# A Trainium2 encoder trunk: decay weights spread over other steps, heads' rows tied to steps, merging in eight banks

## The chip, the cores and the metric

The kernel runs on one core of a Trainium2 chip. The metric is the time of one execution on the device, in microseconds (us). The profile is of one execution of its own; its engines are PE (TensorE), DVE (VectorE), ACT (ScalarE), POOL (GpSimd) and SP (SyncE, which here issues nearly all DMA transfers).

## The reference

Two sequences, of 1024 and of 256 tokens with 1024 channels each, go through one layer with shared weights. In short (the four heads, and the two directions of the mLSTM, are written once):

```python
h = rms_norm(x, norm_g) * (1.0 + scale) + shift          # shift, scale, gate = c @ w_ada + b_ada
cb, cc, cx, cz, q, k, v, o, mz, gpre, gmerge = split_combined(h @ w_in)
y_conv = cb * centred_dwconv3(cc * cx, conv_w, conv_b) * silu(cz)
# mLSTM, in chunks of 128 tokens, forwards and backwards; C, n, m are carried from chunk to chunk
Dlog = where(mask, b[t] - b[s] + i[s], NEG_BIG)            # b: cumulated log of the forget gate
S = (q @ k.T) * exp(Dlog - m_t)
num = S @ v + inter_w * (q @ C)
hm = num / max(abs(den), exp(-m_t))
y_m = sigmoid(o) * rms_norm_per_head(hm_fwd + hm_bwd) * silu(mz)
merged = g_conv * (y_conv @ w_proj_conv) + g_mlstm * (y_m @ w_proj_mlstm)
y = rms_norm(x + gate * (merged @ w_out), final_norm_g)
```

All of it is float32. The kernel reaches that precision by splitting each operand in a high and a low part and summing three products.

## The kernel before

The 1280 tokens are treated together, with the channels on the partitions for the projections. PE's work comes in this order (times from the span's start in the profile):

- **Projections** h @ w_in, until about 1161 us, by a Strassen scheme. `go(k)` does one of some 310 steps: 24 matmuls of 128 x 320 (L810), into an "acc" tile of three PSUM buffers. The step's weights come through `raw` (three buffers, loaded from `w_in`), sums and differences `comb` on DVE (L675) and a split in `wh` on ACT (L320) and `wl` on POOL (L321). DVE empties each product (L719) or ACT copies it (L733). A bank is free again after that.
- Beside them run the gate recurrences (`recurrences`) and, behind those, the **decay weights**: `weights(i)`, 20 of them, at L1243 to L1258. Each is a load of rows of `a_dr` to all partitions, an addition of the mask on POOL (L1251), four exponentials on ACT (L1255) and a store to `ex_dr`. They share four places, two halves of two `big` tiles: `weights(i)` uses the place of `weights(i - 4)`, so its load waits for that store. The loop at L1345 to L1351 sets at which steps they are due. The convolution's steps (`conv_pairs`) come after `ends[8]`.
- **Sweeps**, 1161 to 1446 us, the mLSTM: `Sweep.query` (L1465, qc), `Sweep.state` (L1505, u; L1513 updates C on DVE), scores (L1548) and the rest, 55 loop steps `s`. Between them stand, as filler, 32 units of y_conv @ w_proj_conv (L1713 to L1715, 24 matmuls each; `Filler.unit`), whose weights are loaded and split two units at a time. `load_head(h, n, which)` loads v, q and k of a head in three pieces of 5, 3 and 2 chunks (640, 384 and 256 KB for each of the three).
- **Merging**, 1446 to 1564 us: y_m @ w_proj_mlstm in 16 blocks of two products of 24 matmuls (L1883 to L1885). `merge` takes a PSUM bank for each product, and DVE multiplies it with the gate `th` (L620). The second half of the blocks uses `ym1`, which `second_ym` loads and splits.
- **Final products** with w_out (L1975 to L1977) until the end.

The order of the instructions on each engine is not that of the code. `Board.op` records operations with a duration, a due step (`board.step`), what they wait for, and marks: `low` (when nothing else is ready), `slack` (added to the time at which a result is taken as ready) and `after`. `Board.order` then plays a planned run: it takes the operation that could begin first, and among those within 0.25 us of it the one that is not low and has the earliest step. For a transfer the planned duration is KB divided by `KB_US`. `play()` emits the instructions in this order, one play for the projections, one for the sweeps, one for merging, one for the rest. On the chip each engine works through its own order strictly. SP has eight semaphores in rotation, and its n-th DMA waits until the one eight before it has landed.

Of the kernel before, what the change touches and what calls it, by code (L numbers as in the profile page):

```python
# [9 lines left out]
F32 = mybir.dt.float32  # L10
F32R = mybir.dt.float32r
AF = mybir.ActivationFunctionType
ALU = mybir.AluOpType
# [3 lines left out]
P = 128  # L17
# [165 lines left out]
def encoder_kernel(  # L183
# [1058 lines left out]
    def weights(i):  # L1242

        gx = gcol[:, 0].rearrange("p d h c -> p d (h c)")
        if not weighing:
            weighing.extend(big() for _ in range(2))
        b, c = weighing[i % 2], i // 2 % 2
        place = (b, c)
        abc = (lambda: b[:, c * 4 * P:(c + 1) * 4 * P].rearrange("p (d j s) -> p d j s", d=2, j=2))
        load(256, abc, a_rows[:, 2 * i:2 * i + 2, :].partition_broadcast(P), ["a_dr"], [place])  # L1250
        op("POOL", 1.35, lambda: G.tensor_tensor(out=abc(), in0=abc(), in1=masks[:].unsqueeze(2).to_broadcast([P, 2, 2, P]),  # L1251
                                                 op=ALU.add), r=[place], w=[place], slack=4.0)
        for d in range(2):
            for j in range(2):
                op("ACT", .39, lambda d=d, j=j: A.activation(abc()[:, d, j, :], abc()[:, d, j, :], AF.Exp,  # L1255
                                                             bias=gx[:, d, 2 * i + j:2 * i + j + 1], scale=1.0),
                   r=[place, "pre"], w=[place])
        store(256, ex_dr[i], lambda: b[:, c * 4 * P:(c + 1) * 4 * P], [place])  # L1258


    sts = {n: gate_pair(n, n + 2, max(i - 2, 0), i == 0) for i, n in enumerate((0, 1, 4, 5, 8, 9))}
# [80 lines left out]
    board.step = at[0]  # L1342
    recurrences()

    for n in range(2, KT):  # L1345
        if n > 3:
            for i in range(NH * NC // 2):
                if i * 4 // (NH * NC // 2) == n - 4:
                    board.step = at[0] + 7 * (i * 4 % (NH * NC // 2)) // (NH * NC // 2)
                    weights(i)  # L1350
        advance(ends[n + 1])  # L1351
    advance(ends[9])

    def first_y():
# [32 lines left out]
                b.open = True  # L1387
    board.KB_US, board.FIRST = 385.0, 1.0
    board.play()
    board.KB_US, board.FIRST = Board.KB_US, Board.FIRST  # L1390
    rstack.close()
    sstack.close()
    xstack.close()
# [34 lines left out]
    def piece(c):  # L1428
        return 0 if c < 5 else 1 if c < 8 else 2

    def load_head(h, n, which="qkv", low=True):

        i, (c0, c1) = h % 2, PIECES[n]
        hs, ts_ = slice(h * HD, (h + 1) * HD), slice(c0 * P, c1 * P)
        kb = 128 * (c1 - c0)
        if "v" in which:
            load(kb, lambda: vNs[i][:, c0:c1, 0:HD], v_dr[ts_, hs].rearrange("(c p) d -> p c d", p=P), (), [(vNs[i], n)], low and h > 0)
        for nm, t, src in (("q", qTs[i], qT_dr), ("k", kTs[i], kT_dr)):
            if nm in which:
                load(kb, lambda t=t: t[:, :, ts_], src[hs, ts_].rearrange("(b p) t -> p b t", p=P), (), [(t, n)], low and h > 0)  # L1440

    class Sweep:

# [309 lines left out]
    for s in range(10 * NH + 15):  # L1753
        board.step = s
        if s == 0:
            fills.unit(())
            load_head(0, 2)
        h, c, i = second(s - 3)
        if h is not None and h + 2 < NH and c in (5, 7, 9):
            load_head(h + 2, (5, 7, 9).index(c))  # L1760
        h, i = divmod(s, 10)
        mark = len(board.ops)
        if h < NH:
            c, d = one[h].order[i], one[h].d
            one[h].query(c, lambda h=h, c=c, d=d: kept[h % 2][:, slot(d, c), :], (kept[h % 2], c))
            one[h].state(c)
        if s == 0:
            fills.unit(())
            for n in DOWN[1:]:
                load_head(0, n, "qv")  # L1770
            fills.unit(())
            fills.unit(())
        h, c, i = second(s)
        if h is not None:
            g = c - c % 2
            if i % 2 == 0:
                prs[h, g] = Pairs(h, g, two_[h].d)
            two_[h].query(c, *prs[h, g].inter(c))
            two_[h].state(c)
            prs[h, g].scores(c)  # L1780
            if i % 2:
                prs[h, g].factors()
        h, c, i = second(s - 2)
        if h is not None:
            prs[h, c - c % 2].values(c)
        h, c, i = second(s - 4)
        if h is not None and i % 2 == 0:
            prs[h, c - c % 2].finish()
        if s in (3, 5):
            for h, n in ((0, 0), (1, 2), (1, 1)) if s == 3 else ((1, 0), (0, 1)):  # L1790
                load_head(h, n, "qkv" if h else "k", False)
        after = [o for o in board.ops[mark:] if o.eng == "PE"][:1]
        while fills.at < PACE[s]:
            fills.unit(after)
        if s == 45:
            ym0 = [first_ym(0)]
        if s == 51:
            raws_m = [raw_tile() for _ in range(2)]
            for j, raw in enumerate(raws_m):
                load(512, lambda raw=raw: raw[:], wpm[:, 4 * j:4 * j + 4, 0:2 * P], (), [raw])  # L1800
            ws_m = [split_op(lambda raw=raw: raw[:, :, 0:P], [raw]) for raw in raws_m]
# [8 lines left out]
    bstack.close()  # L1810


    psO = ctx.enter_context(tc.tile_pool(name="psO", bufs=2, space=PSUM))
    psY = hpstack.enter_context(tc.tile_pool(name="psY", bufs=4, space=PSUM))
    mgp = ctx.enter_context(tc.tile_pool(name="mgp", bufs=1))
    zcp = hpstack.enter_context(tc.tile_pool(name="zcp", bufs=5, side="right"))
    def bank():
        b = buf(psY, [P, 512], F32, "acc", 4)
        return b, b

    def mg_half(pool, tags):
# [20 lines left out]
    def second_ym(n):  # L1842
        y = [buf(hp, [P, 4, TH2], F32R, ("b00", "b10")[n] + part, 1) for part in "HL"]
        v = ym_dr[:].rearrange("(k p) t -> p k t", p=P)
        for k in range(4):
            raw = buf(thp, [P, TH2], F32, "th", NTH)
            kt = 4 * n + k
            load(320, lambda raw=raw, kt=kt: raw[:], v[:, kt, 0:TH2], (), [raw], True)
            op("ACT", .8, lambda raw=raw, k=k: A.copy(y[0][:, k], raw[:]), r=[raw], w=[(y[0], k)])
            op("DVE", .83, lambda raw=raw, k=k: V.tensor_tensor(out=y[1][:, k], in0=raw[:], in1=fp(y[0][:, k]),  # L1850
                                                                op=ALU.subtract), r=[raw, (y[0], k)], w=[(y[1], k)])
        return y
# [222 lines left out]
    ym1 = []  # L2075
    for i in range(2 * KT):
        board.step = i
        if i < 6 and i % 2 == 0 and i < 4:
            ym1.append(second_ym(i // 2))
        if i in (5, 7, 9):  # L2080
            n_ = (5, 7, 9).index(i)
            fetch_into((B11, B21, T2)[n_], ("b11", "b21", "t2")[n_], low=True)
        if i + 1 < 2 * KT:
            block_weights(i + 1)
        merge(i, ym0 if i < KT else ym1)
# [19 lines left out]
        b.open = False  # L2105
    hpstack.close()

    psE, psD = (ctx.enter_context(tc.tile_pool(name=nm, bufs=1, space=PSUM)) for nm in ("psE", "psD"))
    og = ctx.enter_context(tc.tile_pool(name="og", bufs=1))
    late = ctx.enter_context(tc.tile_pool(name="late", bufs=3, side="right"))  # L2110
    small = ctx.enter_context(tc.tile_pool(name="small", bufs=2))
# [199 lines left out]
```

## Time and profile before

| | us |
|---|---|
| median of 3 runs | 1673.4 (1671.58 to 1675.62) |
| profiled execution | 1674.54 |
| its span | 1672.8 |
| PE idle, L810 (projections) on DVE L719 | 4.1, two times |
| PE idle, L1883 (merging) on DVE L620 | 3.4, once |
| PE idle, L1465 (sweeps) on DVE L1513 | 2.8, three times |

The profiled execution's own time is its span and 1.7 us around it. The mean granted clock of PE is 0.99. Where a row has something in brackets, that is the time for which the engine stood idle just before it, and what ended the wait. The rows that matter stand in the prediction.

### The profile page before, as it was taken

To read this page: it belongs to the slowest core of one execution; us is meant where nothing else is said; L and a number is where in the kernel's file an instruction comes from. 1 tells how busy PE (TensorE), PEld (TensorE's weight loads), DVE (VectorE), ACT (ScalarE), POOL (GpSimd) and SP (SyncE) were. 2 spreads that over 40 slices of the span, in tenths; PEclk is the share of its full clock that TensorE was granted. 3 is DMA by queue.
4 is the path that set the end of the run, shared out by engine and by line. 5 is a ranking of instruction groups with operands and counts; after the bars stand their busy time and mean duration, and the time that the engine had idled before them with its cause. 6 is when DMAs were issued, how large, how long until landed. Compare 5 with 4: busy or idle time off the path is not lost.

```text
span 1672.8 us, 28179 instructions
## 1 busy us (share of the span) xinstructions
PE 1628.8 (97%) x10504; PEld 1561.2 (93%) x10504; DVE 1027.1 (61%) x1747; ACT 588.8 (35%) x1170; POOL 703.8 (42%) x545
## 2 busy tenths in 40 slices
PE   6999999999999999999999999999899999899998
PEld 3989999999999999999999999999798899899886
DVE  5785555556555565566666786652147778443597
ACT  4643443323554222222222221121246565321232
POOL 2243676623655566677667643333120001244000
PEclk8999999999999999999999999999999999999999
DMA  9434778712554222222222465457958865596554
GB/s 361 130 100 147 227 235 239 212 54 69 153 160 137 59 70 70 83 70 62 59 76 65 138 147 140 117 135 250 360 159 260 277 212 176 199 343 234 198 208 173
DMA packets 310524, 274.41 MB, mean 164 GB/s; under 512 B 98820, under 2 KB 260852, under 8 KB 310388
## 3 DMA queue, kind: packets, MB, share of 16 engines
q1 hardware_dynamic: 310084, 272.35, 52.7%
q8 instruction: 83, 1.36, 0.3%
q14 instruction: 53, 0.43, 0.1%
q10 hardware_dynamic: 304, 0.27, 0.0%
HBM read 186.89 MB, written 85.66 MB: 163 GB/s over the span
## 4 chain that ended last, share of the span: by engine, by line
PE 63%; DMA 3%; DVE 1%; SPq 1%; issue 0%; ACT 0%; POOL 0%; DVEq 0%; POOLq 0%; ACTq 0%
PE acc L810 38%; PE u L1505 3%; PE qc L1465 2%; PE acc L1883 2%; PE acc L1884 2%; PE acc L1885 2%; PE acc L1977 2%; PE acc L1975 2%; PE acc L1976 2%; PE acc L1715 2%; PE acc L1714 2%; PE acc L1713 2%; DMA th<-th_dr 2%; PE misc L1588 1%; PE misc L1548 1%; SPq L309 1%
## 5 line engine op out<-in xcount | busy, mean ns | idle before, releaser
L321 POOL TENSOR_TENSOR wl<-comb,wh 128x512 fp32r<-128x512 f32 x176 | 246.7, 1402 | 263.8 <-ACT wh L320 238.4
L321 POOL TENSOR_TENSOR wl<-raw,wh 128x512 fp32r<-128x512 f32 x168 | 235.1, 1400 | 279.2 <-ACT wh L320 270.0
L719 DVE TENSOR_TENSOR q<-acc,q 128x640 f32<-128x640 f32 x272 | 220.7, 819 | 191.4 <-PE acc L810 183.7
L810 PE MATMUL acc<-xt,wh 128*128 128x320 f32 x1408 | 263.8, 309 | 0.0
L810 PEld LDWEIGHTS acc<-xt,wh 128*128 128x128 f32 x1408 | 220.9, 188 | 0.1
L320 ACT CAST wh<-raw 128x512 fp32r<-128x512 f32 x168 | 103.8, 620 | 325.6 <-PE acc L810 191.8
L320 ACT CAST wh<-comb 128x512 fp32r<-128x512 f32 x176 | 108.9, 619 | 280.9 <-PE acc L810 247.1
L810 PE MATMUL acc<-xt,wl 128*128 128x320 f32 x704 | 160.4, 309 | 0.0
L1671 POOL TENSOR_TENSOR wl<-raw,wh 128x512 fp32r<-128x512 f32 x28 | 35.9, 1288 | 227.7 <-ACT wh L1670 227.4
L810 PEld LDWEIGHTS acc<-xt,wl 128*128 128x128 f32 x704 | 117.7, 188 | 0.0
L675 DVE TENSOR_TENSOR comb<-raw 128x512 f32<-128x512 f32 x88 | 72.9, 828 | 61.0 <-DMA raw<-in_w_in_dram 37.3
L617 ACT ACTIVATE q<-q,zero 128x640 f32<-128x640 f32 x76 | 63.1, 831 | 86.1 <-DVE q L719 79.4
L878 POOL TENSOR_TENSOR big<-big,q 128x640 f32<-128x640 f32 x48 | 78.3, 1632 | 35.6 <-DVE q L719 27.2
L620 DVE SCALAR_TENSOR_TENSOR th<-th,acc 128x320 f32<-128x320 f32 x62 | 30.1, 486 | 100.7 <-PE acc L1885 51.5
L675 DVE TENSOR_TENSOR comb<-raw,comb 128x512 f32<-128x512 f32 x44 | 49.8, 1131 | 58.9 <-POOL wl L321 58.9
L810 PE MATMUL acc<-t3L,wh 128*128 128x320 f32 x352 | 81.5, 313 | 2.7 <-DVE t3L L372 2.7
L810 PE MATMUL acc<-t2H,wh 128*128 128x320 f32 x352 | 80.9, 311 | 2.8 <-DVE q L719 2.8
L810 PE MATMUL acc<-t3H,wh 128*128 128x320 f32 x352 | 81.3, 312 | 1.3 <-ACT t3H L371 1.3
L810 PE MATMUL acc<-b00H,wh 128*128 128x320 f32 x352 | 82.4, 315 | 0.0
L810 PE MATMUL acc<-b10H,wh 128*128 128x320 f32 x352 | 80.8, 311 | 1.3 <-DVE q L719 1.3
L810 PE MATMUL acc<-t3H,wl 128*128 128x320 f32 x352 | 81.3, 313 | 0.0
L810 PE MATMUL acc<-b11H,wh 128*128 128x320 f32 x352 | 81.2, 312 | 0.0
(392 smaller groups left out, 4171.1 us busy)
## 6 DMA issues: line engine op xcount, KB each, us to landing
raw<-in_w_in_dram SPq DMA_DIRECT2D x120, 256.0 KB
raw<-in_w_in_dram SPq DMA_DIRECT2D x34, 512.0 KB
th<-th_dr SPq DMA_DIRECT2D x31, 320.0 KB
th_dr<-q SPq DMA_DIRECT2D x28, 320.0 KB
raw<-in_w_proj_conv_dram SPq DMA_DIRECT2D x16, 512.0 KB
raw<-in_w_proj_mlstm_dram SPq DMA_DIRECT2D x16, 512.0 KB
late<-t_dr SPq DMA_DIRECT2D x16, 512.0 KB
k<-kn_dr SPq DMA_DIRECT2D x56, 128.0 KB
```

The lines of the kernel that those rows point to most:

```text
L320: op("ACT", .63, lambda: A.copy(wh[:], src()), r=r, w=[wh])
L321: op("POOL", 1.4, lambda: G.tensor_tensor(out=wl[:], in0=src(), in1=fp(wh[:]), op=ALU.subtract), r=[*r, wh], w=[wl])
L617: A.activation(out, in_, AF.Tanh, bias=zero[:, 0:1], scale=0.5)
L675: op("DVE", .9, lambda: V.tensor_tensor(out=t[:], in0=x(), in1=y(), op=o), r=[x.tok, y.tok], w=[t])
L719: op("DVE", .82, lambda: V.tensor_tensor(out=two(dst()), in0=acc[:, :, 0:TQ], in1=two(t()), op=ALU.add), r=[acc, t.tok], w=[dst.tok])
L810: PE.matmul(acc[:, q, 0:TQ], st_[:, k_, :], m_[:, q * TQ:(q + 1) * TQ], start=k_ == 0 and n == 0, stop=k_ == 3 and n == 2)
L878: op("POOL", 1.65, lambda: G.tensor_tensor(out=dst(), in0=dst(), in1=t(), op=ALU.mult), r=[dst.tok, t.tok], w=[dst.tok])
L1465: PE.matmul(pq[:, 0:HD + 2], qTs[i][:, kd, c * P:(c + 1) * P], C[:, kd, :], start=kd == 0, stop=kd == 1)
L1505: PE.matmul(pu[:, db, 0:HD + 2], k[:, db * P:(db + 1) * P], wv[:], start=True, stop=True)
L1671: op("POOL", 1.36, lambda wh=wh, wl=wl, src=src: G.tensor_tensor(out=wl[:], in0=src(), in1=fp(wh[:]), op=ALU.subtract), r=[raw, wh], w=[wl])
L1713: PE.matmul(acc[:, :TQ], wh, yH, start=kt == 0, stop=False)
L1714: PE.matmul(acc[:, :TQ], wh, yL, start=False, stop=False)
```

## The change

It has four parts.

1. *Decay weights.* The 20 calls of `weights` were spread from two steps of the og pairs on, five to each of four pairs. Now they are spread evenly from `ends[3] + 3` to `ends[8] - 3`, with `advance` between. The load and the store are planned as 512 and 384 KB in place of 256 (they move what they moved), and the slack of POOL's addition is 3.0 in place of 4.0.
2. *Heads' rows.* `load_head` takes `after` in place of `low`. The pieces of v and q of head 0 that were loaded at step 0 and the rows at steps 3 and 5 are now at steps 1, 4, 6 and 9, and are due after the step's first PE operation in the plan. The planner's rate for the sweeps' play is 290 KB a us in place of 230.
3. *Merging's second operand.* `second_ym` is called at blocks 2 and 4 in place of 0 and 2, and its ACT cast has slack 4.0.
4. *Banks.* The pool of merging's products, `psY`, has eight buffers in place of four. `psO`, the pool of the final products, was opened before it and is opened after it is closed.

```diff
         abc = (lambda: b[:, c * 4 * P:(c + 1) * 4 * P].rearrange("p (d j s) -> p d j s", d=2, j=2))
-        load(256, abc, a_rows[:, 2 * i:2 * i + 2, :].partition_broadcast(P), ["a_dr"], [place])
+        load(512, abc, a_rows[:, 2 * i:2 * i + 2, :].partition_broadcast(P), ["a_dr"], [place])
         op("POOL", 1.35, lambda: G.tensor_tensor(out=abc(), in0=abc(), in1=masks[:].unsqueeze(2).to_broadcast([P, 2, 2, P]),
-                                                 op=ALU.add), r=[place], w=[place], slack=4.0)
+                                                 op=ALU.add), r=[place], w=[place], slack=3.0)
...
-        store(256, ex_dr[i], lambda: b[:, c * 4 * P:(c + 1) * 4 * P], [place])
+        store(384, ex_dr[i], lambda: b[:, c * 4 * P:(c + 1) * 4 * P], [place])
...
-    for n in range(2, KT):
-        if n > 3:
-            for i in range(NH * NC // 2):
-                if i * 4 // (NH * NC // 2) == n - 4:
-                    board.step = at[0] + 7 * (i * 4 % (NH * NC // 2)) // (NH * NC // 2)
-                    weights(i)
-        advance(ends[n + 1])
+    k0, k1 = ends[3] + 3, ends[8] - 3
+    for i in range(NH * NC // 2):
+        advance(k0 + (k1 - k0) * i // (NH * NC // 2))
+        board.step = at[0]
+        weights(i)
     advance(ends[9])
...
-    board.KB_US, board.FIRST = Board.KB_US, Board.FIRST
+    board.KB_US, board.FIRST = 290.0, Board.FIRST
...
-    def load_head(h, n, which="qkv", low=True):
+    def load_head(h, n, which="qkv", after=None):
...
+        def fetch(dst, src, tok):
+            op("SP", kb, lambda: dma(dst(), src), w=[tok], low=h > 0 and after is None, after=after or ())
+
...
-            for n in DOWN[1:]:
-                load_head(0, n, "qv")
+            load_head(0, 1, "qv")
...
-        if s in (3, 5):
-            for h, n in ((0, 0), (1, 2), (1, 1)) if s == 3 else ((1, 0), (0, 1)):
-                load_head(h, n, "qkv" if h else "k", False)
         after = [o for o in board.ops[mark:] if o.eng == "PE"][:1]
+        for h, n, which in {1: ((0, 0, "qv"),), 4: ((1, 2, "qkv"),), 6: ((0, 0, "k"), (1, 1, "qkv")),
+                            9: ((1, 0, "qkv"), (0, 1, "k"))}.get(s, ()):
+            load_head(h, n, which, after)
...
-    psO = ctx.enter_context(tc.tile_pool(name="psO", bufs=2, space=PSUM))
-    psY = hpstack.enter_context(tc.tile_pool(name="psY", bufs=4, space=PSUM))
+    psY = hpstack.enter_context(tc.tile_pool(name="psY", bufs=8, space=PSUM))
...
-            op("ACT", .8, lambda raw=raw, k=k: A.copy(y[0][:, k], raw[:]), r=[raw], w=[(y[0], k)])
+            op("ACT", .8, lambda raw=raw, k=k: A.copy(y[0][:, k], raw[:]), r=[raw], w=[(y[0], k)], slack=4.0)
...
-        if i < 6 and i % 2 == 0 and i < 4:
-            ym1.append(second_ym(i // 2))
+        if i in (2, 4):
+            ym1.append(second_ym(i // 2 - 1))
...
-    psE, psD = (ctx.enter_context(tc.tile_pool(name=nm, bufs=1, space=PSUM)) for nm in ("psE", "psD"))
+    psO, psE, psD = (ctx.enter_context(tc.tile_pool(name=nm, bufs=n, space=PSUM)) for nm, n in (("psO", 2), ("psE", 1), ("psD", 1)))
```

How this moves instructions is seen in the order that the planner gives each engine. Three places matter for the prediction.

**Projections, steps 118 to 122, on DVE.** Rows are line, operation, output and inputs with their numbers, shape. Here `acc_5182` before and `acc_5183` now are the product of step 120, and `comb_5201` and `comb_5249` the first combination of the raw weights loaded last. Before:

```order
L620 SCALAR_TENSOR_TENSOR q_5161<-q_5161,q_5147 128x640
L719 TENSOR_TENSOR q_5103<-acc_5138,q_5103 128x640
L675 TENSOR_TENSOR comb_5201<-raw_5057,raw_5145 128x512
L620 SCALAR_TENSOR_TENSOR q_5203<-q_5203,q_5103 128x640
L620 SCALAR_TENSOR_TENSOR q_5028<-q_5028,q_5203 128x640
L719 TENSOR_TENSOR q_4988<-acc_5182,q_4988 128x640
```

And in the changed kernel:

```order
L620 SCALAR_TENSOR_TENSOR q_5173<-q_5173,q_5145 128x640
L719 TENSOR_TENSOR q_5104<-acc_5138,q_5104 128x640
L620 SCALAR_TENSOR_TENSOR q_5209<-q_5209,q_5104 128x640
L620 SCALAR_TENSOR_TENSOR q_5022<-q_5022,q_5209 128x640
L719 TENSOR_TENSOR q_4982<-acc_5183,q_4982 128x640
L675 TENSOR_TENSOR comb_5249<-raw_5102,raw_5171 128x512
L675 TENSOR_TENSOR comb_5261<-comb_5249,raw_5102 128x512
```

The combination, which waits for both raw tiles, stood ahead of the emptying of step 120's product and now stands behind it. The same happens six steps later. SP's queue at that later place, before, where `big` with `a_dr` is a load of weights and `ex_dr` a store of them:

```order
L309 DMA raw_5350<-in_w_in_dram 128x4x128 x2
L312 DMA ex_dr_69<-big_4601 128x512
L309 DMA big_4609<-a_dr_63 128x2x256
L312 DMA ex_dr_69<-big_4609 128x512
L309 DMA big_4601<-a_dr_63 128x2x256
L309 DMA raw_5417<-in_w_in_dram 128x4x128 x2
L309 DMA big_4609<-a_dr_63 128x2x256
```

And in the changed kernel, with `raw_5373` and `raw_5429` in the place of `raw_5350` and `raw_5417`:

```order
L312 DMA ex_dr_69<-big_4609 128x512
L309 DMA raw_5373<-in_w_in_dram 128x4x128 x2
L309 DMA big_4601<-a_dr_63 128x2x256
L309 DMA big_4609<-a_dr_63 128x2x256
L309 DMA raw_5429<-in_w_in_dram 128x4x128
L312 DMA ex_dr_69<-big_4601 128x512
L309 DMA raw_5429<-in_w_in_dram 128x4x128
```

The second raw pair was behind one load of weights and ahead of another; now both loads, and for its second half a store too, stand between the two pairs.

**Start of the sweeps, on SP.** `raw` with `in_w_proj_conv` are the filler's weights, `vN`, `qT` and `kT` rows of heads, `k` the chunks of k, `abc` and `og` operands of the first scores. Before, in the middle of the first rows (the `kT` of 128x2x640 is of head 0, the rows of `vN`, `qT` and `kT` after it of head 1):

```order
L309 DMA kT<-kT_dr 128x2x640
L309 DMA vN<-v_dr 128x2x256
L309 DMA qT<-qT_dr 128x2x256
L309 DMA kT<-kT_dr 128x2x256
L309 DMA vN<-v_dr 128x3x256
L309 DMA qT<-qT_dr 128x2x384
L309 DMA kT<-kT_dr 128x2x384
L1724 DMA zc_dr<-raw 128x640
L309 DMA th<-th_dr 128x640
L309 DMA k<-kn_dr 128x256 x2
L309 DMA vN<-v_dr 128x5x256
L309 DMA qT<-qT_dr 128x2x640
```

Twenty-three rows after the first of these the filler's weights follow. In the changed kernel they stand here:

```order
L309 DMA og<-og_dr 128x2x256
L309 DMA abc<-ex_dr 128x512
L309 DMA og<-og_dr 128x2x256
L1726 DMA zc_dr<-th 128x640
L1436 DMA vN<-v_dr 128x5x256
L1436 DMA qT<-qT_dr 128x2x640
L309 DMA raw<-in_w_proj_conv_dram 128x4x256 x2
L309 DMA k<-kn_dr 128x256
L309 DMA raw<-in_w_proj_conv_dram 128x4x256
L1726 DMA zc_dr<-th 128x640
L309 DMA k<-kn_dr 128x256
L309 DMA th<-th_dr 128x640
```

All rows of head 1, and two pieces of head 0's kT, are now behind the filler's next weights; of the rows ahead only v and q of head 0's piece of five chunks are left. On PE the filler's units now stand singly between the steps of the sweep.

**Start of merging, on SP.** `th` with `th_dr` are the gates that empty a product, `zc` the other summands, `th` with `ym_dr` the rows of the second operand, `raw` the next blocks' weights. Before:

```order
L309 DMA raw_15398<-in_w_proj_mlstm_dram 128x4x256
L309 DMA raw_15413<-in_w_proj_mlstm_dram 128x4x256
L309 DMA th_15450<-ym_dr_70 128x640
L309 DMA th_15458<-ym_dr_70 128x640
L309 DMA th_15466<-ym_dr_70 128x640
L309 DMA th_15477<-ym_dr_70 128x640
L309 DMA th_15481<-th_dr_72 128x640
L309 DMA b11_15495<-b11_dr_77 128x1024 x2
```

In the changed kernel, from the stage's first load on:

```order
L309 DMA th_15358<-th_dr_72 128x640
L309 DMA zc_15367<-zc_dr_64 128x640
L309 DMA raw_15371<-in_w_proj_mlstm_dram 128x4x256
L309 DMA th_15381<-th_dr_72 128x640
L309 DMA zc_15383<-zc_dr_64 128x640
L309 DMA zc_15391<-zc_dr_64 128x640
L309 DMA raw_15395<-in_w_proj_mlstm_dram 128x4x256
```

The first gates were loaded behind four rows of `ym`, and are now the first of the stage; the rows of `ym` follow eleven loads later.

More of the change, by code (lines that the diff above doesn't have):

```diff
@@ L1435, in load_head @@
         kb = 128 * (c1 - c0)
+        def fetch(dst, src, tok):
+            op("SP", kb, lambda: dma(dst(), src), w=[tok], low=h > 0 and after is None, after=after or ())
         if "v" in which:
-            load(kb, lambda: vNs[i][:, c0:c1, 0:HD], v_dr[ts_, hs].rearrange("(c p) d -> p c d", p=P), (), [(vNs[i], n)], low and h > 0)
+            fetch(lambda: vNs[i][:, c0:c1, 0:HD], v_dr[ts_, hs].rearrange("(c p) d -> p c d", p=P), (vNs[i], n))
         for nm, t, src in (("q", qTs[i], qT_dr), ("k", kTs[i], kT_dr)):
             if nm in which:
-                load(kb, lambda t=t: t[:, :, ts_], src[hs, ts_].rearrange("(b p) t -> p b t", p=P), (), [(t, n)], low and h > 0)
+                fetch(lambda t=t: t[:, :, ts_], src[hs, ts_].rearrange("(b p) t -> p b t", p=P), (t, n))
     class Sweep:
@@ L1817, in bank @@
     def bank():
-        b = buf(psY, [P, 512], F32, "acc", 4)
+        b = buf(psY, [P, 512], F32, "acc", 8)
         return b, b
```

## The prediction

> **What bounds the kernel now.** The page comes first: its span and its line of busy times.
>
> ```profile
> span 1672.8 us, 28179 instructions
> PE 1628.8 (97%) x10504; PEld 1561.2 (93%) x10504; DVE 1027.1 (61%) x1747; ACT 588.8 (35%) x1170; POOL 703.8 (42%) x545
> ```
>
> PE (TensorE) is idle for some 44 us in all, and the change leaves the number of matmuls as it is. So nothing can be won except idle time and slow clock. The view of waits, asked for PE, says which idle time there is (engine, line, what it waited for: us in total, times, longest).
>
> ```profile
> PE acc L810 <- DVE q L719: 4.1, 2, 2.8
> PE acc L1883 <- DVE th L620: 3.4, 1, 3.4
> PE qc L1465 <- DVE C L1513: 2.8, 3, 0.9
> PE u L1505 <- DMA k<-kn_dr: 1.4, 1, 1.4
> PE acc L1713 <- ACT wh L1670: 1.1, 1, 1.1
> PE acc L1715 <- POOL wl L1671: 0.8, 1, 0.8
> ```
>
> These six rows hold 13.6 us, and lie at the three places that the change touches: the decay weights (L719), the start of the sweeps (L1465, L1505, L1713, L1715) and the start of merging (L1883). Windows behind the stalls show a second cost (us, PE busy and its matmuls, granted clock, DMA share, GB/s):
>
> ```profile
> 494.25:497.65 3.40, 3.40 (x15) 0.51 0.54 177
> 497.70:501.10 3.40, 3.40 (x25) 1.00 0.52 200
> 1211.10:1214.50 3.40, 3.40 (x15) 0.50 0.67 212
> 1463.70:1467.10 3.40, 2.94 (x11) 0.50 1.03 399
> ```
>
> (The last window's missing PE time is the end of the stall itself.) After each of the three places PE runs one window of 3.4 us at half clock: 15 matmuls where 25 fit, so 10/25 of 3.4 us, 1.4 us, is lost each time. What can be won is 13.6 + 3 x 1.4 = 17.8 us.
>
> Undisturbed, PE does 275 matmuls in 40 us; a step of the projections or a product of a unit has 24, 3.5 us:
>
> ```profile
> 520.00:560.00 40.00, 40.00 (x275) 40.00 (x274) 23.42 (x27) 14.32 (x27) 19.54 (x14) 1.00 0.33 105
> ```
>
> [...]
>
> **The decay weights, about 440 to 526 us.** VectorE first (start, us, engine, line, tiles, idle before and its releaser), then PE.
>
> ```profile
> 480.17 0.82 DVE L719 TENSOR_TENSOR q<-acc,q 128x640 f32<-128x640 f32 x1
> 489.31 0.69 DVE L675 TENSOR_TENSOR comb<-raw 128x512 f32<-128x512 f32 x1 [8.32 <-DMA raw<-in_w_in_dram]
> ...
> 492.49 0.81 DVE L719 TENSOR_TENSOR q<-acc,q 128x640 f32<-128x640 f32 x1
> ...
> 516.09 0.69 DVE L675 TENSOR_TENSOR comb<-raw 128x512 f32<-128x512 f32 x1 [6.28 <-DMA ex_dr<-big]
> ```
>
> ```profile
> 493.44 0.53 PE L810 MATMUL acc<-t2H,wh 128*128 128x320 f32 x2 [2.75 <-DVE q L719]
> ...
> 517.66 0.53 PE L810 MATMUL acc<-b10H,wh 128*128 128x320 f32 x2 [1.32 <-DVE q L719]
> ```
>
> Twice a combination of raw weights (L675) waits for a load, and the emptying of a product (L719) stands behind it on VectorE, so PE finds no free bank of its three. In the changed order the emptying of acc_5183 stands ahead of the combination at the first place, and likewise at the second. Both stalls of before lose their cause: 2.75 + 1.32 + 1.4 = 5.5 us.
>
> What is late next is the raw load itself. SP's queue:
>
> ```profile
> 480.70 0.97 SPq L309 DMA_DIRECT2D raw<-in_w_in_dram  x2
> ...
> 482.93 0.73 SPq L309 DMA_DIRECT2D big<-a_dr  x1
> ...
> 489.86 0.36 SPq L309 DMA_DIRECT2D big<-a_dr  x1
> ...
> 508.64 0.36 SPq L309 DMA_DIRECT2D big<-a_dr  x1
> 509.11 0.95 SPq L309 DMA_DIRECT2D raw<-in_w_in_dram  x2
> ```
>
> An issue of SP waits in order. A load of weights waits until the store before it from the same place has landed: 489.86 to 508.64 is one turn of a place, 18.8 us. The first raw pair (raw_5171 now) goes behind the load that was issued at 482.93, about 3 us later than 480.70; it lands at about 492. VectorE then has three combinations, one L620 and one L719 to do (about 4 us) before the product that PE needs at 497.7 (no stall: 490.7 + 2 steps of 24 matmuls, 3.5 us each). That just fits.
>
> At the second place raw_5429 stands behind **two** weight loads where it stood behind one. These keep their turn of 18 to 19 us: I expect the pair's second half at 509 to 511 and landed at 515.5 to 517.5 (516.0 before). The emptying that PE needs there (acc of step 127, for step 130) comes three VectorE operations later, at about 518 to 520. PE, unstalled, wants step 130 at 515.3; before, it began it at 517.66 + 3.5 = 521.2. So most of what is won is waited for again, 3 to 5 us of it, and a slow window may follow. The ends are -5.5 us (nothing waits) and +1.5 us (a window more). I take **-1.5 us**: step 130 at about 519.5, nearest to the raw's own row at 509.11.
>
> **The start of the sweeps, 1161 to 1215 us.** The windows; the chain that ended last (start, us, by what); then the issue of the first k on SP, and PE:
>
> ```profile
> 1160.00:1200.00 40.00, 38.10 (x246) 36.51 (x245) 7.33 (x13) 8.44 (x17) 6.66 (x9) 1.00 0.98 337
> 1200.00:1240.00 40.00, 35.32 (x192) 31.92 (x193) 11.27 (x32) 13.59 (x31) 10.12 (x8) 0.96 0.68 222
> ```
>
> ```profile
> 1198.82 7.03 DMA raw<-in_w_proj_conv_dram
> ...
> 1208.54 1.28 POOL wl L1671
> ```
>
> ```profile
> 1171.06 0.96 SPq L309 DMA_DIRECT2D k<-kn_dr  x2
> ```
>
> ```profile
> 1181.05 1.11 PE L1505 MATMUL u<-wv,k 128*128 128x258 f32 x4 [1.40 <-DMA k<-kn_dr]
> ...
> 1195.16 0.61 PE L1548 MATMUL misc<-kT,qT 128*128 128x128 f32 x4
> ```
>
> Transfers are the limit here (share 0.98, 337 GB/s). The next weights of the filling convolution products are issued at 1198.82, behind all rows of head 1. The eighth unit ends at 1195.16, and PE runs the bare chain of steps with 0.9 us gaps until the weights are split. In the changed order 4864 KB (head 1's 3840, and 640 + 384 of kT) go behind these weights: 4.98 MB at 337 GB/s is 14.8 us. They would be issued at about 1184, landed at 1191 and split at 1195, where the ninth unit is wanted at about 1197 (1195.2, less the stall of 1.4, plus the 3.2 us of chain steps now between the units). The margin is 2 us. k loses 1280 KB (3.9 us) of what stood ahead of it and waited 1.4, so that stall goes too. All of it is 2.8 + 1.4 + 1.1 + 0.8 + 1.4 = 7.5 us. The rows that go later are not free: the second window has a third of its DMA time unused, 13 us, just under the 14.8 that move there. I take **-7.0 us**, ends -7.5 and 0.
>
> **The start of merging, 1446 to 1467 us.** SP's queue, VectorE, PE.
>
> ```profile
> 1451.84 3.02 SPq L309 DMA_DIRECT2D th<-ym_dr  x4
> 1455.39 0.32 SPq L309 DMA_DIRECT2D th<-th_dr  x1
> ```
>
> ```profile
> 1460.81 2.48 DVE L1850 TENSOR_TENSOR b00L<-th,b00H 128x640 fp32r<-128x640 f32 x3 [13.66 <-ACT b00H L1849]
> 1463.53 0.49 DVE L620 SCALAR_TENSOR_TENSOR th<-th,acc 128x320 f32<-128x320 f32 x1 [0.24 <-DMA th<-th_dr]
> ```
>
> ```profile
> 1464.16 0.60 PE L1883 MATMUL acc<-y,wh 128*128 128x320 f32 x1 [3.41 <-DVE th L620]
> ```
>
> PE ran dry at 1464.16 - 3.41 = 1460.75, after four products of 3.5 us: the fifth needs one of four banks, and the emptying waits for th, which is issued behind four loads of ym, on a VectorE that waits 13.66 us at a cast of those same loads. Now th is the first load of the stage, ym comes later, and eight banks hold PE for 28 us, to about 1474.7, without any emptying. The 3.4 us and the window go. What could be late instead is the weights of the third block (wanted at 1460.6); their loads have no ym ahead of them now. **-4.8 us**; ends -4.8 and -2.
>
> **The end of merging.** VectorE, and PE's first final product.
>
> ```profile
> 1564.48 0.49 DVE L620 SCALAR_TENSOR_TENSOR th<-th,acc 128x320 f32<-128x320 f32 x1 [2.51 <-PE acc L1885]
> ```
>
> ```profile
> 1564.28 0.39 PE L1975 MATMUL acc<-b,wh 128*128 128x512 f32 x1
> ```
>
> The final products had banks of their own, and PE went on at 1564.28. With eight banks in merging's pool they open only when it closes, after its last emptying: 1564.48 + 0.49 and a hand-over, about 1565.0. **+0.7 us**; ends 0 and +2.1 (a slow window). [...]
>
> Other edits (the planner's rate of 290, slack in casts) change only the order; the middle of the sweeps is the same work in slightly different places: 0, ends -1 and +1.
>
> **Sum**: -1.5 - 7.0 - 4.8 + 0.7 = -12.6 us. The profiled execution took 1674.5 us, 1.1 above the median of 1673.4, so I expect 1661.9 for such a one and 1660.8 for the median: **1661 us**.
>
> **The rivals.** (1) *All of it comes*: the raw pair is in time at the second place: -5.5 - 7.5 - 4.8 + 0.7 = -17.1, 1656.3 us. For it: the combination is one step further from PE's need than before. Against it: the two weight loads ahead. (2) *The filler's weights are still late*: zc stores and k loads that wait for PE stand around them in SP's order, and the second gap stays: 7.0 less, 1667.8 us. (3) *The change does not do what it says*: weights spread from the recurrences to the convolution still come out in the same rhythm, because a place's turn of 18.8 us sets it, and only the order on VectorE differs. This is in the forecast's -1.5. (4) *Slower*: head 1's rows and kT, now tied to steps, stand on SP behind k loads that wait for PE's steps. If a step needs a row whose issue waits for the step before, each piece costs a landing, 7.03 us by the raw's row. With the sweeps' 7.0 lost as well, -5.6 is left; from two such landings on (+14) the kernel is slower, 1682 us. Against it: the first of these rows is wanted some 20 us after its issue.
>
> [...] The trace's two windows speak against it; its chance, 5%, lies inside the forecast's.
>
> **How the numbers follow.** Forecast, 1657.5 to 1665: 0.52. All of it: 0.22. Filler late: 0.13. Nothing left within 0.2% (3.3 us, about what a measurement of this kernel tells from no change): 0.06. Slower: 0.07. Faster is 0.87. The range that leaves out less than 2 in 10 goes from rival 1 with one more us or two (1654) to rival 2 with the merging's lesser end (1670).
>
> **What would show it.** Right: no row of waits for L1883 on th L620; qc L1465 not waiting on C; the windows at some 1211 and 1464 at clock 1.00; a PE wait at L810 for L719 that sits near 515 to 520 us; the first L1975 after the last L620. Wrong: a wait of the convolution units for wh or wl near 1197, rows of head 1 (qT, kT, vN) as releasers of PE, or new waits of merging for wl.

## The result, and the profile after

The changed kernel took 1657.9 us in the median of 4 runs (1656.3 to 1660.4), the kernel before beside it 1674.5 us (1671.6 to 1675.6). The ratio is 0.9905, with a 95% interval of 0.9886 to 0.9924: 13 to 19 us faster. The profiled execution is the slowest of the four, with 1660.44 us and a span of 1658.7, 14.1 us less than before. The page's head and the rows of the view of waits for PE that answer to those of before:

```profile
span 1658.7 us, 28185 instructions
PE 1624.2 (98%) x10504; PEld 1558.1 (94%) x10504; DVE 1029.0 (62%) x1747; ACT 588.7 (35%) x1170; POOL 700.7 (42%) x545
```

```profile
PE misc L1587 <- DVE Pt L1584: 2.2, 2, 1.4
...
PE u L1486 <- DMA kT<-kT_dr: 1.2, 1, 1.2
PE misc L1587 <- DVE og L1640: 1.2, 2, 0.9
PE acc L1716 <- DMA b00L<-yc_drL: 1.1, 2, 0.8
...
PE acc L1975 <- ACT wh L1831: 0.6, 1, 0.6
PE acc L1883 <- DVE th L620: 0.6, 1, 0.6
```

The lines of the sweeps have moved by two (L1505 is L1507 now). All six rows of before are gone, but for 0.6 us of L1883, which is at another place. New are small waits, for kT at the start of the sweeps, for rows of y_conv (b00L) in their middle, and one at each end of merging. Two waits late in the sweeps have grown: for Pt (1.9 us before) and for og (0.3 before). The windows show where the time came from, and one loss (us; then busy time and instructions of PE, weight loads, DVE, ACT and POOL; granted clock, DMA share, GB/s). Three of them before, then five now:

```profile
480.00:520.00 40.00, 35.92 (x233) 35.46 (x233) 16.21 (x20) 17.88 (x44) 21.33 (x17) 0.96 0.56 157
1400.00:1440.00 40.00, 37.36 (x231) 35.11 (x230) 31.89 (x105) 21.88 (x61) 6.64 (x6) 0.96 0.48 159
1440.00:1480.00 40.00, 36.59 (x242) 36.34 (x241) 16.57 (x27) 12.17 (x20) 13.65 (x10) 0.96 0.87 313
```

```profile
480.00:520.00 40.00, 40.00 (x275) 40.00 (x274) 25.24 (x26) 23.38 (x53) 26.66 (x20) 1.00 0.59 177
1160.00:1200.00 40.00, 38.81 (x248) 37.51 (x247) 7.61 (x13) 11.04 (x22) 11.02 (x9) 1.00 1.02 348
1200.00:1240.00 40.00, 40.00 (x237) 36.97 (x236) 21.66 (x64) 20.96 (x49) 6.95 (x6) 1.00 0.71 237
1400.00:1440.00 40.00, 36.54 (x225) 34.60 (x224) 24.70 (x75) 17.35 (x45) 9.02 (x7) 0.91 0.39 123
1440.00:1480.00 40.00, 40.00 (x274) 40.00 (x273) 20.31 (x32) 12.78 (x20) 15.15 (x12) 1.00 1.02 362
```

The slice from 480 to 520 us is full now, as are the one from 1200 and the one from 1440. In the slice from 1400 the granted clock is 0.91: the last steps of the sweeps are followed by 6.8 us at half clock, where before it was one window of 3.4.

By stages, each from its first matmul (L810, the first filler, the first of merging, the first L1975) to that of the next, the last one to its last matmul, in the profiled executions:

| us | before | after | difference | foretold |
|---|---|---|---|---|
| projections | 1130.3 | 1124.3 | -6.0 | -1.5 |
| sweeps (with the wait at merging's first product) | 285.5 | 281.5 | -3.9 | -7.0 |
| merging (with the wait at its end) | 117.8 | 113.7 | -4.1 | -4.8 + 0.7 |
| final products | 100.7 | 100.8 | +0.1 | 0 |

The sum was near, -14.0 to -12.6, because two terms missed in opposite directions, and that is luck. In the medians the gain is 16.6 us, 4.0 more than foretold. The experiments ask why.

### The profile page after: what moved, and what is told of

Its sections match the earlier page's. It is cut to its first block, busy times and chain, and to the rows that moved or that the text cites. A ratio compares the mean times of both kernels' runs of the same rounds, so it can differ in the third digit from the quotient of the medians.

```text
span 1658.7 us, 28185 instructions
## 1 busy us (share of the span) xinstructions
PE 1624.2 (98%) x10504; PEld 1558.1 (94%) x10504; DVE 1029.0 (62%) x1747; ACT 588.7 (35%) x1170; POOL 700.7 (42%) x545
## 3 DMA queue, kind: packets, MB, share of 16 engines
q8 instruction: 83, 1.36, 0.3%
## 4 chain that ended last, share of the span: by engine, by line
PE 94%; DMA 3%; DVE 2%; SPq 0%; issue 0%; ACT 0%; DVEq 0%; ACTq 0%
PE acc L810 64%; PE u L1507 3%; PE qc L1467 3%; PE acc L1883 2%; PE acc L1884 2%; PE acc L1885 2%; PE acc L1716 2%; PE acc L1717 2%; PE acc L1715 2%; PE acc L1975 2%; PE acc L1977 2%; PE acc L1976 2%; PE misc L1550 1%; PE misc L1590 1%; PE misc L439 1%; DMA raw<-in_w_in_dram 1%
## 5 line engine op out<-in xcount | busy, mean ns | idle before, releaser
L719 DVE TENSOR_TENSOR q<-acc,q 128x640 f32<-128x640 f32 x272 | 220.8, 819 | 197.8 <-PE acc L810 193.4
L810 PE MATMUL acc<-xt,wh 128*128 128x320 f32 x1408 | 263.8, 309 | 0.0
L810 PEld LDWEIGHTS acc<-xt,wh 128*128 128x128 f32 x1408 | 220.9, 188 | 0.1
L810 PE MATMUL acc<-xt,wl 128*128 128x320 f32 x704 | 160.4, 309 | 0.0
L810 PEld LDWEIGHTS acc<-xt,wl 128*128 128x128 f32 x704 | 117.7, 188 | 0.0
L675 DVE TENSOR_TENSOR comb<-raw 128x512 f32<-128x512 f32 x88 | 75.3, 856 | 49.9 <-DMA raw<-in_w_in_dram 24.2
L675 DVE TENSOR_TENSOR comb<-raw,comb 128x512 f32<-128x512 f32 x44 | 49.5, 1126 | 56.6 <-POOL wl L321 56.6
L810 PE MATMUL acc<-t3L,wh 128*128 128x320 f32 x352 | 81.5, 313 | 2.7 <-DVE t3L L372 2.7
L810 PE MATMUL acc<-t3H,wh 128*128 128x320 f32 x352 | 81.2, 312 | 1.4 <-ACT t3H L371 1.4
L810 PE MATMUL acc<-b00H,wh 128*128 128x320 f32 x352 | 82.3, 315 | 0.0
L810 PE MATMUL acc<-t3H,wl 128*128 128x320 f32 x352 | 81.2, 312 | 0.0
L810 PE MATMUL acc<-b11H,wh 128*128 128x320 f32 x352 | 81.1, 312 | 0.0
L810 PE MATMUL acc<-b10H,wh 128*128 128x320 f32 x352 | 80.7, 310 | 0.0
L810 PE MATMUL acc<-b00L,wh 128*128 128x320 f32 x352 | 80.5, 310 | 0.0
```

The lines of the kernel that those rows point to most:

```text
L675: op("DVE", .9, lambda: V.tensor_tensor(out=t[:], in0=x(), in1=y(), op=o), r=[x.tok, y.tok], w=[t])
L719: op("DVE", .82, lambda: V.tensor_tensor(out=two(dst()), in0=acc[:, :, 0:TQ], in1=two(t()), op=ALU.add), r=[acc, t.tok], w=[dst.tok])
L810: PE.matmul(acc[:, q, 0:TQ], st_[:, k_, :], m_[:, q * TQ:(q + 1) * TQ], start=k_ == 0 and n == 0, stop=k_ == 3 and n == 2)
```

## The experiments

Each is the kernel before, or the changed one, with one thing different (in the last run two). Times are medians with the ratio to the kernel before and its 95% interval; stage lengths are of the profiled executions.

**Three parts alone.** First the decay weights: the diff's pieces on `weights(i)` and on its calls.

```diff
-    for n in range(2, KT):
...
-                    weights(i)
-        advance(ends[n + 1])
+    k0, k1 = ends[3] + 3, ends[8] - 3
+    for i in range(NH * NC // 2):
+        advance(k0 + (k1 - k0) * i // (NH * NC // 2))
+        board.step = at[0]
+        weights(i)
```

> The kernel before with the decay weights' part of the change alone (calls spread, planned costs and slack); the sweeps and merging are as before. Theory: SP issues the weights' transfers and the raw pairs earlier, the emptying stands ahead of the combination on DVE, and both PE waits on q L719 (2.75 and 1.32 us) and the half-clock window behind the first (1.4 to 1.5 us) go: -5.5 to -6.0 us, and the projections end near 1154.7 us in place of 1160.9. Rival (my prediction's step): raw weights arrive behind two weight loads, PE waits again near step 130: -1.5 us.

1668.5 us, 0.9961 (0.9950 to 0.9973). The sweeps begin at 1155.0, the projections last 1125.6 us (1130.3 before), and the view of waits has no L810 on L719. The theory holds; my step of the prediction does not.

The heads' rows, the diff's pieces on `load_head` and its calls, with the rate:

```diff
-    board.KB_US, board.FIRST = Board.KB_US, Board.FIRST
+    board.KB_US, board.FIRST = 290.0, Board.FIRST
...
+        for h, n, which in {1: ((0, 0, "qv"),), 4: ((1, 2, "qkv"),), 6: ((0, 0, "k"), (1, 1, "qkv")),
+                            9: ((1, 0, "qkv"), (0, 1, "k"))}.get(s, ()):
+            load_head(h, n, which, after)
```

> The kernel before with the heads' rows part alone (load_head with after, rows at steps 1, 4, 6 and 9, the planner's rate 290 in the sweeps). Theory: the gaps at qc L1465 and L1713/L1715 and their half-clock window go (some 7 us), and about 3 us come back in other waits of the sweeps, so the stage lasts 281.5 us in place of 285.5: -4 us. Rival (my prediction's step): nothing comes back, -7 us; then the loss seen in the changed kernel comes from its other parts.

1668.9 us, 0.9965 (0.9950 to 0.9980). The sweeps last 279.8 us, 5.7 less than before. That is between the two theories. It has waits for kT (1.25 us) and b00L (0.8) as the changed kernel has.

Merging's part, both pieces:

```diff
-    psY = hpstack.enter_context(tc.tile_pool(name="psY", bufs=4, space=PSUM))
+    psY = hpstack.enter_context(tc.tile_pool(name="psY", bufs=8, space=PSUM))
...
-        if i < 6 and i % 2 == 0 and i < 4:
-            ym1.append(second_ym(i // 2))
+        if i in (2, 4):
+            ym1.append(second_ym(i // 2 - 1))
```

> The kernel before with merging's part alone (second operand two blocks later, eight banks). Theory: the 3.4 us wait of L1883 on L620 and its window go (-4.8 us), and 0.6 us come back at the first block and 0.6 us at the first final product because all eight banks change hands: -4 us. Rival: what matters in merging depends on the order of the sweeps before it, and alone it gives under 3 us.

1670.4 us, 0.9967 (0.9954 to 0.9980); merging lasts 113.7 us, and both ends have their wait, 0.58 and 0.63 us. The three parts give 0.39 + 0.35 + 0.33 = 1.07%, the whole change 0.95% (0.76 to 1.14): they add up.

**Why the decay weights gave all.** Three kernels. The first has only the planned costs and the slack:

```diff
-        load(256, abc, a_rows[:, 2 * i:2 * i + 2, :].partition_broadcast(P), ["a_dr"], [place])
+        load(512, abc, a_rows[:, 2 * i:2 * i + 2, :].partition_broadcast(P), ["a_dr"], [place])
...
-        store(256, ex_dr[i], lambda: b[:, c * 4 * P:(c + 1) * 4 * P], [place])
+        store(384, ex_dr[i], lambda: b[:, c * 4 * P:(c + 1) * 4 * P], [place])
```

> The kernel before with the planned costs and the slack of the decay weights alone (512 and 384 KB, 3.0); the calls are spread as before. Theory: what counts is the planner's order, in which the emptying of step 120's product stands ahead of the combination; this half gives the same order there, so it gives the whole -5.5 to -6 us. Rival: the spreading of the calls brings the transfers forward, and without it raw weights still come too late at the second place: -4 us or less, with a PE wait on q L719 near 515 us.

1668.0 us, 0.9957 (0.9942 to 0.9972); projections 1123.9 us, no wait on L719. The second has only the spread calls (the diff shown first, without the costs):

> The kernel before with the decay weights' calls spread as in the change, at the planned costs and slack of before. In its order the emptying of steps 120 and 126 stands ahead of the combination on DVE. Theory: whatever gives this order gives the gain: -5.5 to -7 us, no wait of L810 on L719. Rival: the spreading puts more weights between the raw pairs, and one wait near 515 us remains: -3 us.

1669.1 us, 0.9970 (0.9960 to 0.9979); projections 1124.9 us, no wait on L719. So either half is enough. The third leaves the weights as they were, and changes only what stands first on DVE:

```diff
+            late = 2.0 if weighing and board.step < 140 else 0.0
-            op("DVE", .9, lambda: V.tensor_tensor(out=t[:], in0=x(), in1=y(), op=o), r=[x.tok, y.tok], w=[t])
+            op("DVE", .9, lambda: V.tensor_tensor(out=t[:], in0=x(), in1=y(), op=o), r=[x.tok, y.tok], w=[t], slack=late)
```

> The kernel before in which the planner takes a combination's inputs as ready 2 us later while the decay weights run, so that on DVE the emptying of steps 120 and 127 stands ahead of the combination; the weights' calls and costs are as before. Theory: DVE's order alone was what held PE, both waits on q L719 go: -5.5 us. Rival (my prediction's step): the raw weights land as late as before, at 489 and 516 us, and what stands behind the combination is waited for within some steps: PE waits 1 to 4 us near 515 to 525 us, -1.5 to -3 us in all.

1667.8 us, 0.9956 (0.9942 to 0.9970); projections 1124.1 us. Its raw weights came about as late as before: at the first place the combination began at 489.86 us (489.31 before), at the second the pair's second half was issued 1.5 us earlier than before. SP's issue of that second half, then DVE at both places (L720 and L676 here are L719 and L675, one line later):

```profile
508.03 0.45 SPq L309 DMA_DIRECT2D raw<-in_w_in_dram  x1
```

```profile
483.99 0.83 DVE L720 TENSOR_TENSOR q<-acc,q 128x640 f32<-128x640 f32 x1
489.86 0.69 DVE L676 TENSOR_TENSOR comb<-raw 128x512 f32<-128x512 f32 x1 [5.05 <-DMA raw<-in_w_in_dram]
...
510.13 0.82 DVE L720 TENSOR_TENSOR q<-acc,q 128x640 f32<-128x640 f32 x1
514.33 1.15 DVE L676 TENSOR_TENSOR comb<-raw 128x512 f32<-128x512 f32 x1 [3.37 <-issue]
```

The second combination began at 514.33 (516.09 before), but the emptying of step 127 stood ahead of it, at 510.13, and PE did not wait. So DVE's order alone is enough, and the rival falls. In the changed kernel the order did it at the first place. At the second, the emptying of step 126 went ahead of the combination, but that of step 127 stayed behind it, and was in time because the raw pair came earlier there (the rows stand below, with the prediction's step). Earlier raw weights alone, in the old order on DVE, were not run.

**What merging needs.** The second operand later, with four banks, and eight banks, with the second operand as early as before. The diffs are the two pieces shown above, one in each.

> The kernel before with merging's second operand two blocks later alone; four banks as before. Theory: the wait of L1883 on L620 (3.4 us) came from the loads of ym ahead of the gates and from the casts ahead of the emptying on DVE, so it goes with its half-clock window, and no bank changes hands: merging lasts 112.8 us in place of 117.8, -5 us. Rival: four banks run dry at the third block all the same, -2 us or less.

1669.6 us, 0.9970 (0.9957 to 0.9983); merging 112.85 us, and no wait in it.

> The kernel before with eight banks alone; the second operand as early as before. Theory: eight banks cover 28 us from about 1446, and the emptying of before came at 1463.5, 3 us late for four banks, so the wait goes here too, less 0.6 us at each end of the stage: -3.6 us, as if either half of merging's part were enough. Rival: DVE still stands at the casts behind late loads, and PE stops one or two blocks later: 0 to -2 us.

1671.0 us, 0.9974 (0.9963 to 0.9985); merging 113.74 us. VectorE with eight banks, then with the later operand:

```profile
1460.87 2.50 DVE L1849 TENSOR_TENSOR b00L<-th,b00H 128x640 fp32r<-128x640 f32 x3 [13.99 <-ACT b00H L1848]
1463.60 0.49 DVE L620 SCALAR_TENSOR_TENSOR th<-th,acc 128x320 f32<-128x320 f32 x1 [0.23 <-DMA th<-th_dr]
```

```profile
1451.15 0.49 DVE L620 SCALAR_TENSOR_TENSOR th<-th,acc 128x320 f32<-128x320 f32 x1 [3.64 <-DMA th<-th_dr]
...
1454.09 0.49 DVE L620 SCALAR_TENSOR_TENSOR th<-th,acc 128x320 f32<-128x320 f32 x1 [0.50 <-PE acc L1885]
```

With eight banks alone VectorE still stands 13.99 us at the casts, and PE does not mind. With the later operand alone the emptying runs from 1451 on, and four banks do. Either is enough, and the later operand is the cheaper by 0.9 us in the stage, since no bank changes hands. The changed kernel's two waits show that price (the first is counted with the sweeps above; at the second the view names ACT, whose cast ended at 1550.03 us, just after VectorE's last emptying at 1549.99, but with four banks there is no wait):

```profile
1436.36 0.41 PE L1883 MATMUL acc<-y,wh 128*128 128x320 f32 x1 [0.58 <-DVE th L620]
```

```profile
1550.09 0.47 PE L1975 MATMUL acc<-b,wh 128*128 128x512 f32 x1 [0.63 <-ACT wh L1831]
```

The changed kernel with four banks, and `psO` opened where it was:

```diff
-    psY = hpstack.enter_context(tc.tile_pool(name="psY", bufs=8, space=PSUM))
+    psO = ctx.enter_context(tc.tile_pool(name="psO", bufs=2, space=PSUM))
+    psY = hpstack.enter_context(tc.tile_pool(name="psY", bufs=4, space=PSUM))
...
```

> The changed kernel with four banks in merging's pool again, and the final products' pool opened where it was before; the second operand stays two blocks later. Theory: on DVE the emptying of merging's products runs within 0.1 us of their end in the changed kernel (L620 at 1440.18, 1443.71, 1447.25), so four banks are enough; the waits of 0.58 us at the first block and 0.63 us at the first final product go: 1.2 us faster than the changed kernel, -15 to -18 us against before. Rival: eight banks are what holds PE over the first blocks; with four the wait of some 3 us and the half-clock window come back, 3 to 5 us slower than the changed kernel.

1656.3 us, 0.9886 (0.9856 to 0.9916); merging 112.84 us, no wait at either end. The interval overlaps with the changed kernel's, so the gain of some 1.2 us is shown by the two rows that went, not by the times.

**Rows and rate in the sweeps.** The changed kernel with the old rate:

```diff
-    board.KB_US, board.FIRST = 290.0, Board.FIRST
+    board.KB_US, board.FIRST = Board.KB_US, Board.FIRST
```

> The changed kernel with the planner's rate of before (230 KB a us) in the sweeps. In its order PE has three bare steps again (72 filler matmuls in one piece behind them), though the rows of head 1 come late as in the change. Theory: the rate and the moved rows are both needed; the rows alone bring the filler's weights in time, but PE does not use them in time, so the gaps at the chain (about 0.94 us each) come back, the wait for kT at the start (1.2 us) goes: the sweeps last 280 to 283 us, 2 us slower than with 290. Rival: the moved rows are all of the gain, and 230 is as fast as 290 or faster by the kT wait.

1664.4 us, 0.9944 (0.9923 to 0.9966); the sweeps last 285.8 us, as before the change. That is more than my theory said, and its reason was wrong: the gaps at the chain did not come back. From the first filler unit to the thirteenth it takes 58.2 us, no more than with 290 (59.1), where the kernel before took 68.3. The loss is in the middle. The same window of this kernel and of the changed one:

```profile
1275.00:1315.00 40.00, 36.17 (x188) 30.01 (x186) 29.36 (x111) 21.47 (x61) 1.27 (x1) 0.96 0.89 283
```

```profile
1275.00:1315.00 40.00, 38.73 (x225) 34.58 (x224) 27.16 (x99) 21.95 (x62) 2.55 (x2) 1.00 0.88 291
```

188 matmuls stand against 225: with 230 the planner leaves less filler here, PE is idle for 3.8 us in place of 1.3, mostly behind VectorE and ScalarE (L1587 and L1590), and a window at half clock falls in it (0.96). Then the rate alone, on the kernel before:

```diff
-    board.KB_US, board.FIRST = Board.KB_US, Board.FIRST
+    board.KB_US, board.FIRST = 290.0, Board.FIRST
```

> The kernel before with the rate of 290 alone; the heads' rows are loaded as before. Theory: the planner takes the filler's weights as early, but the transfers are the limit and the rows of head 1 stand ahead of them, so PE waits for weights in place of the chain: within 2 us of the kernel before. Rival: the order of PE is what matters, and this gives most of the 6 us of the heads' part.

1673.6 us, 0.9992 (0.9976 to 1.0008): no difference. Its next filler weights were issued at 1200.3 us, as late as before, behind head 1's rows. The moved rows clear the start, the rate the middle. The rate without the rows gives nothing that can be measured. Nor do the rows without the rate, as far as a subtraction shows: the kernel with 230 gains 0.56%, and the decay weights and merging alone give 0.39 + 0.33 = 0.72%.

**A better version.** In the order with 290, the first matmuls with kT stand 12 filler matmuls earlier than with 230, and PE waits for kT:

```profile
1165.86 0.68 PE L1486 MATMUL u<-qT,kT 128*128 128x128 f32 x4 [1.19 <-DMA kT<-kT_dr]
```

With 270 they stand six later. With that rate and four banks:

```diff
-    board.KB_US, board.FIRST = 290.0, Board.FIRST
+    board.KB_US, board.FIRST = 270.0, Board.FIRST
```

> The changed kernel with four banks in merging (as in the earlier run) and the rate of 270 in place of 290. In its order the first matmuls with kT stand six filler matmuls (0.9 us) later, and the filler is spread over the steps as with 290. Theory: the wait for kT at the start of the sweeps (0.8 to 1.2 us) goes, the rest stays: 0.5 to 1 us faster than four banks alone, -18 to -20 us against before. Rival: a rate that is planned lower moves other loads, and new waits in the middle of the sweeps cost as much.

1654.3 us (1653.3 to 1655.5), 0.9883 (0.9863 to 0.9903), about 20 us less than before: the lowest median of all. The wait for kT is down to 0.2 us (0.8 with 290 and four banks), and the sweeps last 277.1 us (277.8). Against four banks alone the times cannot tell it; the shorter wait can.

## Why the prediction was right or wrong

The forecast was 1661 us, and 1657.9 was measured, inside the range and nearer to the first rival (all of it comes, 1656.3). Of the signs named for being right one did not come: there is no wait of L810 for L719 near 515 to 520 us.

*The decay weights: -1.5 foretold, -6.0 measured.* The step that failed is "These keep their turn of 18 to 19 us: I expect the pair's second half at 509 to 511", and before it "The first raw pair (raw_5171 now) goes behind the load that was issued at 482.93, about 3 us later than 480.70". I took issue times of the old trace for a new queue. SP in the changed kernel:

```profile
475.38 0.33 SPq L312 DMA_DIRECT2D ex_dr<-big  x1
...
478.39 0.41 SPq L309 DMA_DIRECT2D raw<-in_w_in_dram  x1
...
479.40 1.59 SPq L309 DMA_DIRECT2D raw<-in_w_in_dram  x1
481.08 5.06 SPq L309 DMA_DIRECT2D big<-a_dr  x2
...
497.50 4.03 SPq L309 DMA_DIRECT2D big<-a_dr  x2
501.65 0.39 SPq L309 DMA_DIRECT2D raw<-in_w_in_dram  x1
...
502.63 1.43 SPq L309 DMA_DIRECT2D raw<-in_w_in_dram  x1
```

The store that went at 481.77 before (behind a weight load and a raw pair) now goes at 475.38, ahead of them, so the load that waits for its landing goes at 481.08 and not at 489.86; the next turn of that place takes 16.4 us, not 18.8. The raw pair's second half is issued between 502.63 and 504.1, not at 509 to 511. DVE then:

```profile
484.61 0.82 DVE L719 TENSOR_TENSOR q<-acc,q 128x640 f32<-128x640 f32 x1
...
509.26 1.29 DVE L675 TENSOR_TENSOR comb<-raw 128x512 f32<-128x512 f32 x1 [3.71 <-DMA raw<-in_w_in_dram]
...
512.06 0.82 DVE L719 TENSOR_TENSOR q<-acc,q 128x640 f32<-128x640 f32 x1
```

The first row is the emptying of step 120, at 492.49 before; the last is the emptying of step 127, at 512.06, where I had 518 to 520 and PE wanted it by 515.3. The part that said what held PE (a combination ahead of the emptying) was right, and the kernel with DVE's order alone shows it. The size is clear of the scatter: in the six profiled executions with the old order of the projections they lasted 1128.9 to 1133.0 us, in the eight others 1123.8 to 1125.6.

*The start of the sweeps: -7.0 foretold, -3.9 for the stage.* That the filler's weights come forward was right in mechanism and margin: their issue is in the first row below (1184 was foretold, for a stage that now begins 6.2 us earlier), and the ninth unit began without a wait, in the second.

```profile
1176.55 1.59 SPq L309 DMA_DIRECT2D raw<-in_w_proj_conv_dram  x2
```

```profile
1191.19 0.50 PE L1715 MATMUL acc<-b00H,wh 128*128 128x320 f32 x1
```

All gaps of before at L1465, L1713 and L1715 went. The stage can be cut where the 201st of its matmuls other than filler begins, behind 360 filler matmuls in both kernels. Up to there it took 101.9 us before and 93.1 now: -8.8, more than foretold. The rest took 183.6 and 188.4: +4.8, with PE idle for 6.8 us in place of 4.3 and 6.8 us at half clock in place of 3.4. So the step that failed here is "the middle of the sweeps is the same work in slightly different places: 0, ends -1 and +1".

What came back: kT 1.2 us, still in the first part, since the new rate puts the first matmuls with kT 12 filler matmuls earlier; b00L 1.1 us, rows issued at 1267.18 and 1272.09, beside rows of head 2 (what made them late was not tested); about 1.2 us more behind og and Pt; 0.6 at merging's first product, since eight banks include those of the sweeps' last product (I had priced only the end); and a second window of half clock. The new sweeps lasted 279.8, 281.5 and 277.8 us in three profiled executions (the heads' part alone, the changed kernel, four banks), the old ones 283.3 to 287.5 in eight (285.4 in the mean), so against that mean this term is -4 to -8 us, and -7.0 lay within. The rate of 290, which I costed at nothing ("change only the order"), decides it: without it no gain of this part is left.

*Merging: -4.8 and +0.7 foretold, -4.1 in sum measured.* Both right in place and size. The prediction credited eight banks and the later operand together; either was enough alone. The window behind a stall costs 1.5 us and not 1.4: in it matmuls of 128 x 320 begin 0.27 us apart (before, 1431.14 to 1432.74 us), elsewhere 0.147 (before, 1422.44 to 1423.91 us), so 12.8 begin in 3.41 us where 23.3 would. The counts of 15 and 25 include matmuls that overlap a window's edge.

*The rival on the slower side* (head 1's rows waited for on SP) did not come: the only row of a head that releases PE in the view of waits is the kT of 1165.86 us, and head 1's rows are issued from 1183.68 on.

*The chance of 5% inside the forecast's* rests on a term for the clock that no run shows. What the runs showed in its place is half clock for 3.4 us behind stalls of 2.75 us (before, 493.44 us) and 1.86 us (merging's part alone), and none behind one of 3.29 us (the rate alone); the rows of the last two stand in the last section.

## What to carry to other kernels

When an engine that empties products also does work that waits for loads, its order decides: put what frees a bank ahead of what waits for a transfer, and a load as late as before no longer holds the matmuls (a combination begun at 489.86 us in place of 489.31, and no wait on L719). When a queue is reordered, do not carry the old issue times over: follow the chain of landings anew from the first moved transfer (a store at 475.38 us in place of 481.77 brought the load behind it from 489.86 to 481.08). And before paying for more buffers, ask whether the consumer's queue, not the buffer count, made them run out (merging lasted 112.85 us with four banks and the later operand, 113.74 with eight banks alone).

## What the runs showed that was not expected

I had counted half-clock windows by the stalls ahead of them, and the runs do not bear that out. Without a window stayed a stall of 3.29 us (the rate alone), while one of 1.86 us (merging's part alone) had one:

```profile
492.77 0.54 PE L810 MATMUL acc<-t2H,wh 128*128 128x320 f32 x2 [3.29 <-DVE q L719]
```

```profile
492.80:496.20 3.40, 3.40 (x23) 3.40 (x24) 2.59 (x4) 3.40 (x9) 0.31 (x1) 1.00 0.61 177
```

```profile
492.41 0.78 PE L810 MATMUL acc<-t2H,wh 128*128 128x320 f32 x2 [1.86 <-DVE q L719]
```

```profile
492.51:495.91 3.40, 3.40 (x13) 3.40 (x14) 2.51 (x4) 3.40 (x10) 0.38 (x1) 0.50 0.46 153
```

The first two rows are of one kernel, the last two of the other: after 3.29 us the clock is 1.00, after 1.86 us it is 0.50 for 3.4 us. The end of the sweeps, with waits of 0.91, 0.35 and 1.36 us, had 6.8 us at half clock in the changed kernel; before, with waits of 0.34, 0.36 and 1.94 us, it had 3.4. In these two traces all changes of the granted clock lie on one grid of 3.41 us each. In the kernel before, slow windows begin, among other times, at 494.30, 1211.10, 1429.55 and 1463.69 us, which are 210, 64 and 10 steps apart; in the changed one, at 94.78 and 1415.74 us, 387 steps apart. The same two stalls by steps of 3.41 us, laid so that a slow window of their own traces (from 518.34 us with the rate alone, from 492.51 us with merging's part alone) is a step:

```profile
487.62:491.03 3.41, 1.86 (x13) 1.00 0.20 66
491.03:494.45 3.42, 1.68 (x11) 1.00 0.63 171
494.45:497.86 3.41, 3.41 (x26) 1.00 0.40 136
```

```profile
489.10:492.51 3.41, 1.55 (x11) 1.00 0.74 71
492.51:495.92 3.41, 3.41 (x13) 0.50 0.45 152
```

The stall of 3.29 us is split between two steps, which are idle for 1.55 and 1.74 us; that of 1.86 us lies whole in one. In the traces of before and of the changed kernel, from 60 us on to 20 us before the end, each of the 7 steps at full clock with 1.61 to 2.94 us of idle PE was followed by a slow one, and none of the 911 with 1.32 us or less was; the step with 1.74 us above was not. For a prediction it means, as an estimate from these rows, 0, 1.5 or 3 us (no, one or two windows) for stalls of 2 to 4 us in all; that executions of one kernel scatter by as much was not shown.
